# Output projection: four token tiles through both column halves, then the other four

## The chip, the core and the metric

The kernel runs on one core of a Trainium2 chip. The core has five engines that run side by side, each through its own list of instructions in order: TensorE (PE, matrix multiply; PEld is its weight load), VectorE (DVE), ScalarE (ACT), GpSimd (POOL), and SyncE (SP), which here issues every DMA. They wait for each other by semaphores. The metric is the device time of one execution in microseconds; three runs of the kernel before gave 1167.01 us in the median (1166.46 to 1168.68).

## The reference

One encoder block over 1024 tokens of width 1024, in float32:

```
n   = rms_norm(x, attn_norm_w)
y   = [ windowed attention with sink (8 heads) || bidirectional retention (8 heads) ] of n @ w_in
h   = x + y @ w_out                       # the output projection
m   = rms_norm(h, ffn_norm_w)
out = h + (silu(m @ w_gate) * (m @ w_up)) @ w_down
```

## The kernel before

**Split operands.** Every float32 operand of a large matmul is split into a high part (rounded) and a low part (what is left), and each product is three matmuls: high by high, high by low, low by high. So each block of weights (a granule, 128x512, 256 KB) is loaded by DMA into a tile `raw`, cast into `wh` (line 224), and `wl` = `raw` - `wh` is subtracted (line 229). Which engines do it is two letters: `W_MID` = "ap" is the cast on ACT and the subtraction on POOL; `W_HOLD` = "pd", used during attention, is POOL and DVE. There are 7 `raw` buffers and 10 pairs of `wh` and `wl`; a pair is free again when the last token tile that needs its granule has been through (line 272).

**The output projection.** The 1024 tokens are 8 tiles of 128. `w_out` has two halves of 512 columns, (O, 0) and (O, 1), with 8 granules each. A pass is one tile through one half: 8 granules of 3 matmuls, accumulated in one of three PSUM banks (names `o0_4`, `o1_4`: half 0 and 1 of tile 4). Before, all 8 tiles go through half 0, then all 8 through half 1, in the order `PAIRED` = 0, 4, 1, 5, 2, 3, 6, 7. `residual` (line 803) adds `x`, writes `h` to HBM and lets ACT sum the squares.

**The norm.** After a tile's second half `norm_rows` (line 837) forms the scale `hr` (DVE, DVE, POOL power), scales both halves of `h` on DVE, transposes them on PE (`pm`), and writes what the gate and up products read. Tiles 0 to 3 are copied to `stash` and split into `X_hi`, `X_lo`. Tile t of 4 to 7 is combined with tile t - 4 into the sums of Winograd's variant of Strassen's scheme: `t1` (in `stash`), `t2`, `t3`, `b22` and `t4`, split into `X` and the tiles T2, T3 and T4. `t4` and the low part of T4 are POOL's (lines 870 and 873), all other sums DVE's.

**Order.** A scheduler lays the instructions out at compile time by priority and a cost model; each engine then runs its list in order. The loop at line 1009 interleaves the projection with the norms: `fill` (line 285) lets PE do projection steps in between, `drain(prev)` puts in the transposes and sums of the tile before. `prepare` loads and splits the first gate and up weights (`A11`, `A12`, sums `S1` to `S4`). After it the products begin: `pa` and `pb` (A11, A12 against tiles 0 to 3), then `pa` with T2, `pc`, `pa` with T3, `pc`, `pa` with T4.

Of the kernel before, what the change touches and what calls it, by code (L numbers as in the profile page):

```python
# [12 lines left out]
ALU = mybir.AluOpType  # L13
# [6 lines left out]
NT = S // P  # L20
# [8 lines left out]
AX_BUFS = 5  # L29
W_FIRST = ("pp", "dd") * 4  # L30
W_MID = "ap"
W_HOLD = "pd"
ENG = {"a_rope": "d", "r_rope": "d", "a_vz": "d", "a_rv": "d", "a_kh": "a", "a_vh": "a", "a_kl": "d", "a_vl": "d",
       "a_kv": "a", "scan": "d", "r_vh": "a", "r_Rh": "da", "r_Rl": "pd", "r_vl": "p", "r_gw": "p", "r_qkh": "a",
# [2 lines left out]
       "o_c": "a", "o_h": "p", "o_l": "p", "y_h": "d", "m_h": "da"}  # L37
FILL = {"A": 2, "Aend": 7, "B1": 2, "B2": 5, "C1": 4, "C2": 4, "D0": 6, "D1": 2, "T1": 3, "O0": 4, "O1": 4, "O2": 3}
SOONER = {"w": -80, "exp": 10, "pass": 0}
PAIRED = (0, 4, 1, 5, 2, 3, 6, 7)  # L40
LEAD = 6
DOWN_LEAD = 5
RD_BUFS = 10
# [17 lines left out]
def hymba_block(ctx, tc, x, xT, cst, prm, retw, ffnw, wqkv, wkv, wout, wg, wu, wd, out):  # L61
# [35 lines left out]
    pe, act, dve, pool = (Engine(e) for e in (nc.tensor, nc.scalar, nc.vector, nc.gpsimd))  # L97
# [33 lines left out]
    def f32(ap):  # L131
        return ap.bitcast(F32)
# [4 lines left out]
    def mm_ps(name):  # L137
        return pp.tile([P, 512], F32, name=name, tag="mm", bufs=MM_BUFS)
# [15 lines left out]
    def four(v):  # L154
        return v[:].rearrange("p (j n) -> p j n", n=P)
# [32 lines left out]

    A, B, C, D, O = "a", "b", "c", "d", "o"
    src = {(A, 0): wqkv[0], (B, 0): wqkv[1], (A, 1): wqkv[2], (B, 1): wqkv[3], (C, 0): wkv, (D, 0): wqkv[4],  # L190
           (O, 0): wout[0], (O, 1): wout[1]}
    chunks = list(src)
    granules, first_granule = [], {}
    for c in chunks:
# [2 lines left out]
    seq = []  # L197
    for c in chunks:
        n = WIDE if seq else 3
        ts = PAIRED if c == (O, 1) else range(NT)  # L200
        seq += [(c, t, k) for k in range(8) for t in ts[:n]] + [(c, t, k) for t in ts[n:] for k in range(8)]
    W = []
    pos = [0]
# [1 line left out]
    hold = [False]  # L205
# [5 lines left out]
    def load_next():  # L211
        with sooner("w"):
            load_granule()

    def load_granule():
        i = len(W)
        raw = wp.tile([P, 512], F32, name=f"raw{i}", tag="raw", bufs=RAW_BUFS)
        hi = wp.tile([P, 512], F32R, name=f"wh{i}", tag="wh", bufs=W_BUFS)
        lo = wp.tile([P, 512], F32R, name=f"wl{i}", tag="wl", bufs=W_BUFS)
        nc.sync.dma_start(raw[:], granules[i])  # L220
        mode = W_FIRST[i] if i < 8 else W_HOLD if hold[0] else W_MID
        e1, e2 = mode
        if e1 == "a":
            act.copy(hi[:], raw[:])
        elif e1 == "d":
            dve.tensor_copy(hi[:], raw[:])
        else:
            pool.tensor_scalar(hi[:], raw[:], 1.0, 1.0, op0=ALU.mult, op1=ALU.mult)
        (dve if e2 == "d" else pool).tensor_tensor(lo[:], raw[:], f32(hi[:]), op=ALU.subtract)
        W.append((hi, lo))  # L230
# [12 lines left out]
    def sip():  # L243

        c, t, k = seq[pos[0]]
        per = 2 if c[0] == C else 1
        g = first_granule[c] + k // per
        i = part[0]
        if i == 0:
            while len(W) <= g:  # L250
                load_next()
            if c == chunks[0] and t == 0:
                split_x(k, 0)
            if k == 0:
                banks[c, t] = mm_ps(f"{c[0]}{c[1]}_{t}")
                begun[0] += 1
        width = 512 // per
        o = (k % per) * width
        lh, ll = (X[:, k, t * P:t * P + P] for X in (X_hi, X_lo))
        rh, rl = (w[:, o:o + width] for w in W[g])  # L260
        with sooner("pass"):
            pe.matmul(banks[c, t][:, :width], ll if i == 2 else lh, rl if i == 1 else rh,
                      start=k == 0 and i == 0, stop=k == 7 and i == 2)
        part[0] = (i + 1) % 3
        if i < 2:
            return
        pos[0] += 1
        if c == chunks[0] and t == 3:
            split_x(k, 1)
        if k == 7:  # L270
            done.add((c, t))
        if t == NT - 1 and (k + 1) % per == 0:
            freed[0] = g + 1
        if not hold[0] and pos[0] % PUMP == 0:
            pump(1)
# [9 lines left out]
    def fill(n):  # L285

        n = round(3 * n)
        while n and ready():
            sip()
            n -= 1  # L290

    def need(c, t):
        while (c, t) not in done:
            sip()
        return banks[c, t]
# [9 lines left out]
    def split_x(k, half):  # L305

        xv = xs[:, xcount[0] % 8, :]
        xcount[0] += 1
        nc.sync.dma_start(xv, xT[k][:, half * 512:half * 512 + 512])
        xh, xl = (X[:, k, half * 512:half * 512 + 512] for X in (X_hi, X_lo))  # L310
        act.activation(xh, xv, AF.Copy, scale=anw[:, k:k + 1])
        dve.scalar_tensor_tensor(xl, xv, anw[:, k:k + 1], f32(xh), op0=ALU.mult, op1=ALU.subtract)
# [209 lines left out]
    def drain(gen):  # L522
        for _ in gen:
            pass
# [7 lines left out]
    for g in range(2):  # L532
# [3 lines left out]
        prev = iter(())  # L536
        for t in range(NT):
            ps = need((A, g), t)
# [16 lines left out]
            prev = gen  # L555
# [5 lines left out]
        for c in range(NT):  # L561
            ps = need((B, g), c)
# [167 lines left out]
    prev = iter(())  # L730
    for t in range(NT):
        ps = need((C, 0), t)
# [9 lines left out]
        prev = gen  # L742
# [31 lines left out]
    for i in range(2 * NT):  # L774
        t, kv = divmod(i, 2)
# [26 lines left out]

    def residual(t, ch, xr, h):
        nc.sync.dma_start(xr[:], x[t * P:(t + 1) * P, ch * 512:ch * 512 + 512])
        ps = need((O, ch), t)
        dve.tensor_tensor(h[:], ps[:], xr[:], op=ALU.add)
        took()
        nc.sync.dma_start(Hd[t][ch][:], h[:])
        act.activation(xr[:], h[:], AF.Square, accum_out=hss[:, t, ch:ch + 1])

    for t in range(NT):
        residual(t, 0, U(f"xr{t}", TAG["xr"]), U(f"h{t}", "y"))
        fill(FILL["O0"])
    front.close()
# [13 lines left out]
    def T_(name, tag):  # L828
        return p2.tile([P, 512], F32, name=name, tag=tag, bufs=MID[tag])

    stash = {}

    def split_to(hi, lo, v, e_lo=None):
        act.activation(hi, v, AF.Copy)
        (e_lo or dve).tensor_tensor(lo, v, f32(hi), op=ALU.subtract)

    def norm_rows(t, h, hn):

        dve.tensor_tensor(hr[:, t:t + 1], hss[:, t, 0:1], hss[:, t, 1:2], op=ALU.add)
        dve.tensor_scalar(hr[:, t:t + 1], hr[:, t:t + 1], 1.0 / DM, EPS, op0=ALU.mult, op1=ALU.add)  # L840
        pool.tensor_tensor(hr[:, t:t + 1], hr[:, t:t + 1], mhalf[:, 0:1], op=ALU.pow)
        for a in range(2):
            dve.scalar_tensor_tensor(hn[a][:], h[a][:], hr[:, t:t + 1], ffnw_t[:, a * 512:a * 512 + 512],
                                     op0=ALU.mult, op1=ALU.mult)
        yield
        pts = []
        for a in range(2):
            pt = ax_ps(f"pm{t}_{a}")
            for j in range(4):
                pe.transpose(pt[:, j * P:j * P + P], hn[a][:, j * P:j * P + P], f32(ident[:]))  # L850
            pts.append(pt)
        if t < 4:
            for a in range(2):
                b = T_(f"stash{t}{a}", "four")
                act.activation(b[:], pts[a][:], AF.Copy)
                stash[t, a] = b
                split_to(*x_rows(t, 4 * a), four(pts[a]))
            return
        u = t - 4
        b11, b21 = stash[u, 0], stash[u, 1]  # L860
        t1, t4 = b11, b21
        b22, t2, t3 = (T_(f"{v}_{u}", "five") for v in ("b22", "t2", "t3"))
        to = lambda i: tuple(TT[i][:, v, :, u * P:u * P + P] for v in range(2))
        act.activation(b22[:], pts[1][:], AF.Copy)
        dve.tensor_tensor(t1[:], pts[0][:], b11[:], op=ALU.subtract)
        dve.tensor_tensor(t2[:], pts[1][:], t1[:], op=ALU.subtract)
        dve.tensor_tensor(t3[:], b22[:], pts[0][:], op=ALU.subtract)
        split_to(*to(2), four(t2))
        split_to(*x_rows(t, 0), four(t1))
        pool.tensor_tensor(t4[:], b21[:], t2[:], op=ALU.subtract)  # L870
        split_to(*to(3), four(t3))
        split_to(*x_rows(t, 4), four(b22))
        split_to(*to(4), four(t4), pool)


    def split(name, v):
# [129 lines left out]
        finish(unit, 1, 0, b1[:], None)  # L1006

    prev = iter(())
    for t in PAIRED:
        h = [T_(f"h{t}_{ch}", "four_") for ch in range(2)]  # L1010
        nc.sync.dma_start(h[0][:], Hd[t][0][:])
        xr = T_(f"xr{t}_1", "five")
        residual(t, 1, xr, h[1])
        gen = norm_rows(t, h, (h[0], xr))
        go(gen)
        if t == PAIRED[-2]:
            prepare(2)
        fill(FILL["O1"])
        drain(prev)
        fill(FILL["O2"])  # L1020
        prev = gen
# [82 lines left out]
    for i in range(4):  # L1104
        h = pd.tile([P, 512], F32, name=f"h21{i}", tag="hd", bufs=8)
# [70 lines left out]
```

## Time and profile before

| what | value |
|---|---|
| median of 3 runs | 1167.01 us |
| the profiled execution, its own time | 1167.41 us |
| span of its profile | 1165.6 us |
| PE busy | 1128.6 us (97%) |
| DVE busy | 833.0 us (71%) |
| ACT busy | 548.2 us (47%) |
| POOL busy | 248.2 us (21%) |
| mean granted clock of TensorE | 0.991 |

The projection's matmuls run from 401.9 to 524.0 us, the first of them between those of attention, which ends at about 452 us. From 555 us on PE is busy in 606.8 of 610.6 us. An operation's duration in the trace includes its fill, so matmuls that follow each other closely are read by the distance of their starts.

### The profile page before, as it was taken

To read this page: it belongs to the slowest core of one execution; us is meant where nothing else is said; L and a number is where in the kernel's file an instruction comes from. 1 tells how busy PE (TensorE), PEld (TensorE's weight loads), DVE (VectorE), ACT (ScalarE), POOL (GpSimd) and SP (SyncE) were. 2 spreads that over 40 slices of the span, in tenths; PEclk is the share of its full clock that TensorE was granted. 3 is DMA by queue.
4 is the path that set the end of the run, shared out by engine and by line. 5 is a ranking of instruction groups with operands and counts; after the bars stand their busy time and mean duration, and the time that the engine had idled before them with its cause. 6 is when DMAs were issued, how large, how long until landed. Compare 5 with 4: busy or idle time off the path is not lost.

```text
span 1165.6 us, 16106 instructions
## 1 busy us (share of the span) xinstructions
PE 1128.6 (97%) x5384; PEld 928.2 (80%) x5384; DVE 833.0 (71%) x1632; ACT 548.2 (47%) x1134; POOL 248.2 (21%) x308
## 2 busy tenths in 40 slices
PE   8989998998999999998999999999999999999998
PEld 6767787787978887876888888888888888888887
DVE  6988876888889994589766676677657755555553
ACT  4744544445478874346334333433333334454441
POOL 3345734358545631322000000000000000000000
PEclk9989999999999999999999999999999999999999
DMA  8520112003100023631534554456445768776672
GB/s 288 200 73 1 37 37 62 12 1 91 37 1 2 19 73 109 192 115 55 188 120 153 190 173 134 136 181 188 144 120 173 231 217 278 232 231 190 216 266 71
DMA packets 82594, 152.59 MB, mean 131 GB/s; under 512 B 9424, under 2 KB 9936, under 8 KB 82512
## 3 DMA queue, kind: packets, MB, share of 16 engines
q1 hardware_dynamic: 82512, 151.57, 40.6%
q8 instruction: 42, 0.69, 0.2%
q14 instruction: 40, 0.33, 0.1%
HBM read 111.43 MB, written 40.11 MB: 130 GB/s over the span
## 4 chain that ended last, share of the span: by engine, by line
PE 70%; DVE 16%; issue 5%; POOL 5%; DMA 3%; ACT 1%; SPq 0%; POOLq 0%; DVEq 0%; ACTq 0%
PE pa L88 20%; PE da L88 10%; PE pc L88 10%; PE dc L88 5%; PE pb L88 5%; PE a L88 4%; PE o L88 4%; PE db L88 3%; PE d L88 3%; PE c L88 1%; DVE X_lo L88 1%; PE b L88 1%; POOL Y L88 1%; DMA xs<-in_xT_dram 1%; DVE h L88 1%
## 5 line engine op out<-in xcount | busy, mean ns | idle before, releaser
L91 POOL TENSOR_TENSOR wl<-raw,wh 128x512 fp32r<-128x512 f32 x44 | 60.0, 1389 | 60.8 <-ACT wh L91 60.4
L88 PE MATMUL b<-wh,X_hi 128*128 128x512 f32 x128 | 53.8, 420 | 0.0
L88 PE MATMUL b<-wh,X_lo 128*128 128x512 f32 x128 | 52.7, 412 | 0.0
L88 PE MATMUL a<-wh,X_lo 128*128 128x512 f32 x128 | 51.1, 400 | 1.7 <-DVE X_lo L88 1.6
L88 PE MATMUL a<-wh,X_hi 128*128 128x512 f32 x128 | 50.7, 396 | 1.9 <-DVE krv L88 1.9
L88 PE MATMUL b<-wl,X_hi 128*128 128x512 f32 x128 | 52.1, 407 | 0.0
L88 PE MATMUL o<-wh,X_hi 128*128 128x512 f32 x128 | 51.1, 399 | 0.0
L88 PE MATMUL a<-wl,X_hi 128*128 128x512 f32 x128 | 50.9, 397 | 0.0
L88 PE MATMUL o<-wh,X_lo 128*128 128x512 f32 x128 | 50.2, 392 | 0.0
L88 PE MATMUL o<-wl,X_hi 128*128 128x512 f32 x128 | 50.1, 392 | 0.0
L88 DVE TENSOR_TENSOR S<-A,A 128x512 f32<-128x512 f32 x44 | 31.3, 711 | 3.1 <-DMA A<-in_wg_dram 2.2
L91 ACT CAST wh<-raw 128x512 fp32r<-128x512 f32 x44 | 26.2, 616 | 10.1 <-PE o L88 4.6
L88 PEld LDWEIGHTS a<-wh,X_lo 128*128 128x128 f32 x128 | 24.3, 190 | 7.9 <-DVE X_lo L88 3.4
L88 PEld LDWEIGHTS a<-wh,X_hi 128*128 128x128 f32 x128 | 24.2, 189 | 6.9 <-issue 2.5
L88 PEld LDWEIGHTS b<-wh,X_lo 128*128 128x128 f32 x128 | 25.1, 196 | 5.3
L88 ACT ACTIVATE sg<-sg 128x512 f32<-128x512 f32 x33 | 20.8, 631 | 17.7 <-DVE sg L88 17.7
L88 PEld LDWEIGHTS b<-wl,X_hi 128*128 128x128 f32 x128 | 25.5, 199 | 4.4
L88 PEld LDWEIGHTS b<-wh,X_hi 128*128 128x128 f32 x128 | 25.7, 201 | 4.0
L88 PEld LDWEIGHTS a<-wl,X_hi 128*128 128x128 f32 x128 | 24.4, 190 | 4.7 <-DVE wl L88 0.4
L88 PEld LDWEIGHTS o<-wh,X_lo 128*128 128x128 f32 x128 | 24.0, 188 | 4.6
L88 PEld LDWEIGHTS o<-wh,X_hi 128*128 128x128 f32 x128 | 24.1, 188 | 4.4
L88 PEld LDWEIGHTS o<-wl,X_hi 128*128 128x128 f32 x128 | 24.1, 188 | 4.2
(2950 smaller groups left out, 3786.3 us busy)
## 6 DMA issues: line engine op xcount, KB each, us to landing
A<-in_wg_dram SPq DMA_DIRECT2D x44, 256.0 KB, 2.9
A<-in_wu_dram SPq DMA_DIRECT2D x44, 256.0 KB, 3.1
R<-in_wd_dram SPq DMA_DIRECT2D x44, 256.0 KB, 2.7
L_S<-LS SPq DMA_DIRECT2D x44, 256.0 KB, 2.3
R_T<-RT SPq DMA_DIRECT2D x44, 256.0 KB, 2.1
raw<-in_wqkv_dram SPq DMA_DIRECT2D x40, 256.0 KB, 2.9
L_A<-a SPq DMA_DIRECT2D x33, 256.0 KB, 2.3
xs<-in_xT_dram SPq DMA_DIRECT2D x16, 256.0 KB, 5.2
```

The costliest lines, as they stand in the source:

```text
L88: ins = fn(*args, **kw)
L91: ins = fn(*args, **kw)
```

## The change

Tiles 0, 4, 1, 5 (`EARLY`) go through both halves first, then 2, 3, 6, 7 (`LATE`). The list of chunks becomes (O, 0) and (O, 1) for `EARLY`, (O, 2) and (O, 3) for `LATE`, where (O, 2) is half 0 and (O, 3) half 1 again: 32 granules in place of 16, so 16 more DMAs, casts and subtractions. All splits of these granules outside attention are now "ad": the cast on ACT, the subtraction on DVE. And `t4` and the low part of T4 move from POOL to DVE. The passes and the order of the norms (0, 4, 1, 5, 2, 3, 6, 7) stay.

```diff
+W_OUT = "ad"
-PAIRED = (0, 4, 1, 5, 2, 3, 6, 7)
+EARLY, LATE = (0, 4, 1, 5), (2, 3, 6, 7)
...
-           (O, 0): wout[0], (O, 1): wout[1]}
+           (O, 0): wout[0], (O, 1): wout[1], (O, 2): wout[0], (O, 3): wout[1]}
+
+    tiles = {c: (EARLY, EARLY, LATE, LATE)[c[1]] if c[0] == O else tuple(range(NT)) for c in src}
...
-        mode = W_FIRST[i] if i < 8 else W_HOLD if hold[0] else W_MID
+        mode = W_FIRST[i] if i < 8 else W_HOLD if hold[0] else W_OUT if i >= first_granule[O, 0] else W_MID
...
-        if t == NT - 1 and (k + 1) % per == 0:
+        if t == tiles[c][-1] and (k + 1) % per == 0:
...
-        ps = need((O, ch), t)
+        ps = need((O, ch + 2 * (t in LATE)), t)
...
-    for t in range(NT):
+    for t in EARLY:
         residual(t, 0, U(f"xr{t}", TAG["xr"]), U(f"h{t}", "y"))
...
-        pool.tensor_tensor(t4[:], b21[:], t2[:], op=ALU.subtract)
+        dve.tensor_tensor(t4[:], b21[:], t2[:], op=ALU.subtract)
...
-        split_to(*to(4), four(t4), pool)
+        split_to(*to(4), four(t4))
...
-    for t in PAIRED:
+    for t in EARLY + LATE:
+        if t == LATE[0]:
+            for u in LATE:
+                residual(u, 0, T_(f"xr{u}_0", "five"), T_(f"h{u}_0", "four_"))
+                fill(FILL["O1"])
+                drain(prev)
+                fill(FILL["O2"])
```

In the lists of instructions below, `o1_5` is half 1 of tile 5, `o2_2` half 0 of tile 2 (chunk (O, 2)) and `o3_2` its half 1; `wh64`, `wl64` are granule 64; helper lines 88 and 91 are 89 and 92 in the changed kernel.

DVE, the norms of tiles 4 and 5, before:

```order
L88 TENSOR_TENSOR stash00_5658<-pm4_0_5704,stash00_5658 128x512
L88 TENSOR_TENSOR t2_0_5715<-pm4_1_5709,stash00_5658 128x512
L88 TENSOR_TENSOR t3_0_5716<-b22_0_5714,pm4_0_5704 128x512
L88 TENSOR_TENSOR X_lo_94<-stash00_5658,X_hi_93 128x4x128
L88 TENSOR_TENSOR T2_5436<-t2_0_5715,T2_5436 128x4x128
L88 TENSOR_TENSOR T3_5437<-t3_0_5716,T3_5437 128x4x128
L88 TENSOR_TENSOR X_lo_94<-b22_0_5714,X_hi_93 128x4x128
L88 TENSOR_TENSOR h5_1_5742<-o1_5_5691,xr5_1_5744 128x512
```

The same place of DVE's list in the changed kernel:

```order
L89 TENSOR_TENSOR stash00_5546<-pm4_0_5604,stash00_5546 128x512
L92 TENSOR_TENSOR wl63_5600<-raw63_5598,wh63_5599 128x512
L89 TENSOR_TENSOR t2_0_5615<-pm4_1_5609,stash00_5546 128x512
L89 TENSOR_TENSOR t3_0_5616<-b22_0_5614,pm4_0_5604 128x512
L89 TENSOR_TENSOR X_lo_94<-stash00_5546,X_hi_93 128x4x128
L89 TENSOR_TENSOR T2_5312<-t2_0_5615,T2_5312 128x4x128
L89 TENSOR_TENSOR stash01_5550<-stash01_5550,t2_0_5615 128x512
L89 TENSOR_TENSOR T3_5313<-t3_0_5616,T3_5313 128x4x128
L89 TENSOR_TENSOR X_lo_94<-b22_0_5614,X_hi_93 128x4x128
L89 TENSOR_TENSOR T4_5314<-stash01_5550,T4_5314 128x4x128
L89 TENSOR_TENSOR h5_1_5648<-o1_5_5579,xr5_1_5650 128x512
```

The two sums of POOL (`stash01`, T4) and a weight split now stand in DVE's list, ahead of the next tile's residual.

DVE, from the residual of tile 2 to that of tile 3, both of half 1, before:

```order
L88 SCALAR_TENSOR_TENSOR xr2_1_5800<-h2_1_5798,hr_5201,ffnw_t_2983 128x512
L88 TENSOR_TENSOR stash10_5780<-pm5_0_5826,stash10_5780 128x512
L88 TENSOR_TENSOR t2_1_5837<-pm5_1_5831,stash10_5780 128x512
L88 TENSOR_TENSOR t3_1_5838<-b22_1_5836,pm5_0_5826 128x512
L88 TENSOR_TENSOR X_lo_94<-stash10_5780,X_hi_93 128x4x128
L88 TENSOR_TENSOR T2_5436<-t2_1_5837,T2_5436 128x4x128
L88 TENSOR_TENSOR T3_5437<-t3_1_5838,T3_5437 128x4x128
L88 TENSOR_TENSOR X_lo_94<-b22_1_5836,X_hi_93 128x4x128
L88 TENSOR_TENSOR h3_1_5864<-o1_3_5813,xr3_1_5866 128x512
```

The same two residuals in the changed kernel:

```order
L89 TENSOR_TENSOR S4_00_6181<-A12_00_6033,S2_00_6151 128x512
L89 TENSOR_TENSOR h2_1_5916<-o3_2_5881,xr2_1_5918 128x512
L89 TENSOR_TENSOR hr_5201<-hss_5200 128x1
L89 TENSOR_SCALAR hr_5201<-hr_5201 128x1
L89 SCALAR_TENSOR_TENSOR h2_0_5915<-h2_0_5915,hr_5201,ffnw_t_2983 128x512
L89 SCALAR_TENSOR_TENSOR xr2_1_5918<-h2_1_5916,hr_5201,ffnw_t_2983 128x512
L89 TENSOR_TENSOR h3_1_5960<-o3_3_5937,xr3_1_5962 128x512
```

The seven sums of tile 5 between them have moved ahead, past the four passes of chunk (O, 2).

PE, the start of chunk (O, 2) in the changed kernel, where the granules of half 0 are needed for the second time:

```order
L89 MATMUL o2_2_5663<-wh63_5599,X_lo_94 128x512
L89 MATMUL pm1_0_5682<-ident_75,h1_0_5563 128x128 x4
L89 MATMUL pm1_1_5687<-ident_75,xr1_1_5566 128x128 x4
L89 MATMUL o2_2_5663<-wh64_5642,X_hi_93 128x512
L89 MATMUL o2_3_5736<-wh60_5481,X_hi_93 128x512
L89 MATMUL o2_3_5736<-wl60_5482,X_hi_93 128x512
L89 MATMUL o2_3_5736<-wh60_5481,X_lo_94 128x512
L89 MATMUL o2_3_5736<-wh61_5496,X_hi_93 128x512
L89 MATMUL o2_3_5736<-wl61_5497,X_hi_93 128x512
L89 MATMUL o2_2_5663<-wl64_5643,X_hi_93 128x512
```

Here the pass of tile 3 starts before that of tile 2 is through; before, passes were not interleaved in this part of PE's list. The first four pairs of `pm` stand about 100 rows earlier in PE's list than before, the last four where they stood.

## Rows read from the trace of the kernel before

**Rows 1.** The page: busy time by engine, and what went to and from HBM.
```profile
PE 1128.6 (97%) x5384; PEld 928.2 (80%) x5384; DVE 833.0 (71%) x1632; ACT 548.2 (47%) x1134; POOL 248.2 (21%) x308
...
HBM read 111.43 MB, written 40.11 MB: 130 GB/s over the span
```

**Rows 2.** Windows: start:end, length, busy us (instructions) by engine, PE clock, DMA share, GB/s.
```profile
504.00:520.00 16.00, 14.48 (x72) 11.79 (x70) 12.56 (x20) 7.64 (x17) 4.27 (x5) 1.00 0.36 118
520.00:531.00 11.00, 8.84 (x37) 6.62 (x38) 10.11 (x20) 8.63 (x19) 0.55 (x1) 0.84 0.23 73
531.00:555.00 24.00, 21.70 (x98) 17.06 (x97) 21.70 (x33) 13.79 (x24) 6.34 (x5) 1.00 0.17 55
```

**Rows 3.** Chain of waits, 440 to 520 us: start, length, what, xcount.
```profile
450.12 28.39 PE o L88 x125
```

**Rows 4.** Timeline of PE, 505 to 562 us: start, length, operation, [idle before <-releaser].
```profile
511.99 0.60 PE L88 MATMUL pm<-ident,h 128*128 128x128 f32 x4
...
512.78 0.48 PE L88 MATMUL o<-wh,X_hi 128*128 128x512 f32 x1
...
518.10 0.39 PE L88 MATMUL o<-wh,X_lo 128*128 128x512 f32 x1
520.30 0.63 PE L88 MATMUL pm<-ident,h 128*128 128x128 f32 x4 [1.82 <-ACT X_hi L88]
...
523.97 0.39 PE L88 MATMUL o<-wh,X_lo 128*128 128x512 f32 x1
525.22 0.66 PE L88 MATMUL pm<-ident,h 128*128 128x128 f32 x4 [0.87 <-DVE h L88]
...
527.69 0.80 PE L88 MATMUL pa<-X_lo,A_00h 128*128 128x512 f32 x1 [0.86 <-DVE X_lo L88]
...
530.42 0.63 PE L88 MATMUL pa<-X_lo,A_00h 128*128 128x512 f32 x1
...
535.87 0.63 PE L88 MATMUL pm<-ident,xr 128*128 128x128 f32 x4 [0.70 <-DVE xr L88]
...
543.70 0.50 PE L88 MATMUL pa<-T,S_00h 128*128 128x512 f32 x1 [1.35 <-DVE T L88]
...
554.89 0.73 PE L88 MATMUL pa<-T,A_00h 128*128 128x512 f32 x2 [0.24 <-DVE sg L88]
```

**Rows 5.** Timeline of DVE at the same columns, attention's end and 505 to 562 us.
```profile
448.02 1.29 DVE L91 TENSOR_TENSOR q71pl<-q71p,q71ph 128x512 fp32r<-128x512 f32 x2 [2.20 <-ACT q71ph L91]
...
512.69 1.41 DVE L88 TENSOR_TENSOR X_lo<-stash,X_hi 128x512 fp32r<-128x512 f32 x1
514.02 2.37 DVE L88 TENSOR_TENSOR T<-t,T 128x512 fp32r<-128x512 f32 x2
...
516.92 0.68 DVE L88 TENSOR_TENSOR h<-o,xr 128x512 f32<-128x512 f32 x1
...
519.40 0.75 DVE L88 SCALAR_TENSOR_TENSOR h<-h,hr,ffnw_t 128x512 f32<-128x512 f32 x1 [0.66 <-POOL hr L88]
...
526.95 1.28 DVE L88 TENSOR_TENSOR X_lo<-pm,X_hi 128x512 fp32r<-128x512 f32 x2
...
528.75 0.68 DVE L88 TENSOR_TENSOR h<-o,xr 128x512 f32<-128x512 f32 x1
...
542.97 0.68 DVE L88 TENSOR_TENSOR T<-t,T 128x512 fp32r<-128x512 f32 x1
```

**Rows 6.** Timeline of POOL, 505 to 562 us.
```profile
512.26 1.29 POOL L88 TENSOR_TENSOR stash<-stash,t 128x512 f32<-128x512 f32 x1 [2.92 <-DVE t L88]
514.29 1.56 POOL L88 TENSOR_TENSOR T<-stash,T 128x512 fp32r<-128x512 f32 x1 [0.74 <-ACT T L88]
```

**Rows 7.** Groups by form, 440 to 560 us: operation xcount | busy, mean ns | idle before.
```profile
L91 POOL TENSOR_TENSOR wl<-raw,wh 128x512 fp32r<-128x512 f32 x6 | 8.4, 1447 | 15.1 <-ACT wh L91 15.1
...
L91 ACT CAST wh<-raw 128x512 fp32r<-128x512 f32 x6 | 3.4, 617 | 4.7 <-PE o L88 4.6
```

**Rows 8.** DMA issues: operation xcount, KB each, median us to landing.
```profile
raw<-in_wout_dram SPq DMA_DIRECT2D x16, 256.0 KB, 2.8
```

More of the change, by code (lines that the diff above doesn't have):

```diff
@@ L199, in hymba_block @@
         n = WIDE if seq else 3
-        ts = PAIRED if c == (O, 1) else range(NT)
+        ts = tiles[c]
         seq += [(c, t, k) for k in range(8) for t in ts[:n]] + [(c, t, k) for t in ts[n:] for k in range(8)]
@@ L831, in hymba_block, with split_to @@
     stash = {}
-    def split_to(hi, lo, v, e_lo=None):
+    def split_to(hi, lo, v):
         act.activation(hi, v, AF.Copy)
-        (e_lo or dve).tensor_tensor(lo, v, f32(hi), op=ALU.subtract)
+        dve.tensor_tensor(lo, v, f32(hi), op=ALU.subtract)
     def norm_rows(t, h, hn):
@@ L1015, in hymba_block @@
         go(gen)
-        if t == PAIRED[-2]:
+        if t == LATE[2]:
             prepare(2)
```

## The prediction

> **What bounds the kernel now.** I read the busy times first: PE is busy for 97% of the span [rows 1], so a change pays only where PE waits or runs slowly. The windows show where that is: three stretches between 504 and 555 us, in which PE is busy for 45.0 us of 51, one of them at a granted clock of 0.84, so partly at 1.2 of 2.4 GHz; DVE is busy for 44.4 us there, in the middle for 10.1 of 11 [rows 2]. The chain of waits gives the pace without waits: 125 matmuls of the projection in 28.39 us [rows 3], 0.227 each, so 5.45 us for a pass of 24.
>
> PE's timeline says what it waits for [rows 4]. From the transposes at 511.99 to the product with T4 at 554.89 us are 42.90 us. The work in it is 132 matmuls (24 + 12 + 24 + 24 + 48) by 0.227, which is 30.0, and four pairs of transposes by 0.79 (511.99 to 512.78), which is 3.2: together 33.1. So 9.8 us are lost. The waits listed are 1.82, 0.87, 0.86, 0.70, 1.35 and 0.24, 5.8 in all; 1.4 is the slow clock (six matmuls from 527.69 to 530.42 take 2.73 in place of 1.36, after PE had waited three times in 10 us); the rest is slow transposes and restarts at the waits.
>
> These waits end with DVE, or with ACT behind DVE. The pass of tile 3 through half 1 ends at 509.3 us (12 matmuls before the transposes at 511.99), but DVE adds its residual only at 516.92 [rows 5], since the sums of tile 5 stand ahead of it in DVE's list. The last pass ends at 524.2; its residual comes at 528.75, 4.5 us late. DVE carries a backlog from tile 5 into the last four norms.
>
> **The change, part by part.** *The norms of tiles 0, 4, 1, 5 move ahead of four passes.* PE's list keeps its passes and transposes; the first four pairs of transposes stand earlier, the last four where they were. In DVE's list the seven sums of tile 5 no longer stand between the residuals of tiles 2 and 3: chunk (O, 2), four passes, lies between. I price a sum or split on DVE at 0.60 (two X_lo and one more fill 526.95 to 528.75 [rows 5]) and count from T, the start of `o1_5`. DVE has `wl67` done at T + 17.1 (below), then ten operations to the residual of tile 3 (T + 23.1), then it waits for PE; `wl70` to `wl75` follow the release of their buffers until T + 31.0, and seven operations, residual and gate weights, end at T + 35.2. PE ends `o3_2` at T + 36.2: 6.2 for `o1_5` with a pair of transposes, five passes, two pairs, 1.1 of waits. So DVE meets the last four norms without a backlog.
>
> *The last four norms* I walk from E, the end of `o3_7`. The residual of tile 6 comes as its pass ends, at E - 6.2; squares, `hr` and scalings take 3.9, two splits and two X_lo 2.4: X_lo of tile 3 is there at E, PE wants it at E + 1.0, so the waits at 525 and 527 go, and that at 520 for the same reason a pass earlier. The scaled tile 7 follows at E + 5.3 (one split in hand, five sums, two scalings by 0.67, two tiny ones, 0.2 for POOL); PE wants it at 0.79 + 5.45 = E + 6.2: the wait at 535 goes. T2 of tile 7 is 14 sums later, E + 13.7; PE wants it at 6.2 + 0.79 + 5.45 + 0.23 = E + 12.6. So a wait of 1.1 stays at T2, between 0 (if 0.54 is the pace) and 2.5 (if each takes the 0.68 that one lasts alone). The wait for `sg` goes, since DVE's list now has it ahead of the next unit's first sum. Gain in this stretch: 9.8 - 1.1 = 8.7, at full clock, as the one wait left is shorter than that of 1.35 at 543.70, after which the clock held [rows 2, 4].
>
> *t4 and the low part of T4 go from POOL to DVE*, two operations by 0.60 for each of four tiles. POOL's two, of 1.29 and 1.56 [rows 6], cost DVE more: beside them one X_lo takes 1.41 in place of 0.68, and two T take 2.37 in place of 1.28 [rows 5], 1.8 together. So 1.2 replaces 1.8. This is already in the walk, which has no POOL work but `hr`.
>
> The Trainium skill ("SBUF — State Buffer", section "Who interferes with whom") says that a VectorE operation with two SBUF inputs and a GpSimd operation that reads SBUF shut each other out for a whole instruction. By that rule DVE would lose up to 1.29 + 1.56 = 2.85 for a tile and the move would gain 1.65, not 0.6; the rows bear out two thirds of it.
>
> *16 more granules.* At the end of attention 54 and 55 are split while DVE stands idle for 2.20 us [rows 5]; their two casts (617 ns each [rows 7]) stand ahead of the ACT copy for which DVE waits there: 0.4 us of delay, between 0 and 0.8. From half 1 to (O, 2) it is tight. Granules 62 to 67 come free one by one during `o1_5`, with the sums of tile 4 between them on DVE. Up to `wl64` DVE has 14 operations by 0.60, two scalings, two tiny ones, and about 1.6 us of waits for the freed buffer, the squares and POOL's power (0.66 [rows 5]): T + 11.7. PE wants `wl64` after 42 matmuls and two pairs of transposes, T + 11.1: a wait of 0.7 with the semaphore. Then the scaled half of tile 5 is 0.3 late and `wl66` 0.15. Together 1.15, between 0 and 3 (14 operations at 0.68 add 1.1, a second late granule the rest). At the step to (O, 3) `wl75` is done at T + 31.0 and PE reaches it at T + 34. POOL's subtractions of 1447 ns [rows 7] go; nothing waits for it then. Granules 44 and 45 put two splits more on DVE before attention and take two from POOL: 0, between -0.5 and 1.2.
>
> *The loads.* 16 DMAs of 256 KB, landing in 2.8 us [rows 8], stand in SP's list between the loads of `x` and `h`. Seven raw buffers run ahead and hide them; the tightest is granule 69, whose issue stands behind a load of `h` that waits for the transposes of tile 4: landing at T + 7, cast at T + 8.7. Without that cover each late load costs PE up to 2.8.
>
> **The sum.** -8.7 + 1.15 + 0.4 = -7.15 us. The profiled execution took 1167.41 (1165.6 of span and 1.8 around it), so 1160.3; the median is 0.4 below that execution, so 1160.0 rounded. After 555 us PE's work follows without gaps, so nothing there gives it back.
>
> **The rivals.**
>
> A. *No new wait at the granules and none at T2:* -9.8, so 1157.2. For it: the walk misses by tenths. Against: DVE's list is dense there.
>
> B. *DVE stays late at the end.* Only the first two waits go (from 518.3 to 520.30 and 524.2 to 525.22, 3.0 together [rows 4]), the three more sums in the last chain add 1.8 at T2 and the granules cost 1.55: +0.35, so 1167. For it: the residual that is 4.5 us late now. Against: tile 5, which makes it late, is out of the way.
>
> C. *The granules make DVE the bound in the middle: slower.* The place is `h1_1` to `wl67`, with 20 sums and splits between PE and its weights. Were they as slow as those beside POOL, three in 3.78, so 1.26 each [rows 5], they would take 13.2 us more, and PE would wait for all of it: 1173. It decides for slower from 9.3 us of waits on, 0.46 more on each. Against: POOL has no sum then.
>
> D. *The traffic bounds.* 16 by 262144 bytes are 4.2 MB, at the mean of 130 GB/s [rows 1] 32 us, so 1199. Against: the DMA share is 0.17 to 0.36 in the three stretches [rows 2]. The Trainium skill ("SBUF — State Buffer", section "A bandwidth-pool intuition that's wrong") says that HBM is almost always the bottleneck from end to end; PE's 97% speaks against it here.
>
> **How the numbers follow.** Forecast 0.64, with its own range of 1158 to 1163.5 (the terms at their ends, or 1.4 us of slow clock at the new waits), A 0.12, B 0.14, C 0.08, D 0.02. The range of 1157.4 to 1166.3 takes in nearly all of A and the lower part of B. No change means within 0.2%, 2.3 us, about what a measurement of this kernel can tell. Faster: the forecast, A and a little of B, 0.80; same: the rest of B, 0.11; slower: C and D but for a mild C, 0.09.
>
> **What would show it.** PE without a wait of over 0.3 us before the transposes of tiles 2, 3, 6 and 7; one of about 1 us at T2 and one of about 0.7 at `wl64`; DVE at 0.60 a sum with nothing on POOL but `hr`; a granted clock near 1.0 from 440 to 560 us. I would be wrong if PE waits for `wl` at most granules, if the residual of tile 7 is late again, or if the clock falls in the middle.

## The result and the profile after

| | us, median | lowest to highest | runs |
|---|---|---|---|
| before | 1167.51 | 1166.46 to 1168.68 | 4 |
| after | 1160.58 | 1160.23 to 1161.78 | 4 |

The ratio is 0.9942, with a 95% interval of 0.9925 to 0.9959. The profiled execution of after took 1161.78 us, 1.2 above the median, of which 1160.0 are its span. Part of that arose where the two kernels still do the same: at 305 us PE stands 1.04 us behind the execution of before (the transposes `k5pt` begin at 306.15 against 305.11). So the two traces differ by less than the medians do (5.6 against 6.9 us), and I compare stretches.

The page (as in [rows 1]) shows 32 more operations on DVE (the splits of 16 more granules, those of 8 granules that POOL had before, and POOL's 8 operations for t4 and T4), 16 fewer on POOL, and 4.2 MB more read:
```profile
PE 1127.6 (97%) x5384; PEld 929.2 (80%) x5384; DVE 841.7 (73%) x1664; ACT 557.0 (48%) x1150; POOL 226.8 (20%) x292
...
HBM read 115.62 MB, written 40.11 MB: 134 GB/s over the span
```
The windows of after (columns as in [rows 2]; the last is cut at the product with T4, 5.5 us earlier than before):
```profile
480.00:504.00 24.00, 22.98 (x105) 18.63 (x104) 21.50 (x38) 13.43 (x28) 0.55 (x1) 1.00 0.76 247
504.00:520.00 16.00, 16.00 (x77) 13.32 (x76) 8.82 (x17) 4.46 (x10) 1.10 (x2) 1.00 0.52 173
520.00:531.00 11.00, 11.00 (x59) 9.23 (x58) 10.23 (x21) 9.37 (x20) 1.10 (x2) 1.00 0.13 47
531.00:549.40 18.40, 17.70 (x81) 14.19 (x80) 18.12 (x31) 12.15 (x20) 0.00 (x0) 1.00 0.22 72
```
PE is busy without a gap from 504 to 531 us, where it lost 3.7 us in [rows 2], and the granted clock is 1.00 throughout. What it lost anew is in the first row: 1.0 of 24 us. The timeline of PE in after, against [rows 4], says where:
```profile
450.57 0.39 PE L92 MATMUL q71o<-q71pl,V 128*128 128x512 f32 x1
...
455.79 0.50 PE L89 MATMUL o<-wl,X_hi 128*128 128x512 f32 x1 [0.49 <-DVE wl L92]
...
482.04 0.50 PE L89 MATMUL o<-wl,X_hi 128*128 128x512 f32 x1 [1.02 <-DVE wl L92]
...
514.56 0.60 PE L89 MATMUL pm<-ident,h 128*128 128x128 f32 x4
...
520.90 0.60 PE L89 MATMUL pm<-ident,h 128*128 128x128 f32 x4
...
524.54 0.60 PE L89 MATMUL pm<-ident,h 128*128 128x128 f32 x4
...
525.65 0.40 PE L89 MATMUL pa<-X_lo,A_00h 128*128 128x512 f32 x1
...
531.32 0.60 PE L89 MATMUL pm<-ident,xr 128*128 128x128 f32 x4
...
538.82 0.50 PE L89 MATMUL pa<-T,S_00h 128*128 128x512 f32 x1 [0.63 <-DVE T L89]
...
549.42 0.62 PE L89 MATMUL pa<-T,A_00h 128*128 128x512 f32 x2
```
The four pairs of transposes and the first X_lo have no bracket any more: nothing is waited for. Three waits are left, at `wl57` (44 matmuls ahead of the first transposes, at 465.90), at `wl64` and at T2 of tile 7. I cut this part of the program in two with such rows. The *middle* runs from the last `q71o` of attention (450.57 here) to the transposes of tile 2 (514.56), the *tail* from there to the product with T4 (549.42). In before the middle begins with this row:
```profile
449.73 0.39 PE L91 MATMUL q71o<-q71pl,V 128*128 128x512 f32 x1
```
Middle and tail took 62.26 (449.73 to 511.99) and 42.90 us there [rows 4], in after 63.99 and 34.86: -8.04 + 1.73 = -6.3 us.

DVE in after, against [rows 5]:
```profile
453.35 4.79 DVE L92 TENSOR_TENSOR wl<-raw,wh 128x512 fp32r<-128x512 f32 x6
462.02 0.69 DVE L89 TENSOR_TENSOR h<-o,xr 128x512 f32<-128x512 f32 x1 [3.87 <-DMA xr<-in_x_dram]
...
481.31 0.68 DVE L92 TENSOR_TENSOR wl<-raw,wh 128x512 fp32r<-128x512 f32 x1
...
518.37 0.69 DVE L89 TENSOR_TENSOR h<-o,xr 128x512 f32<-128x512 f32 x1 [0.38 <-PE o L89]
...
538.09 0.68 DVE L89 TENSOR_TENSOR T<-t,T 128x512 fp32r<-128x512 f32 x1
```
The residual of tile 6 (518.37) now waits for PE: DVE is on time. The second row was not expected: the residual of tile 0 waits 3.87 us for a load.

### The profile page after: what moved, and what is told of

The parts are those of the page before. It is cut to its first block, busy times and chain, and to the rows that moved or that the text cites. A ratio compares the mean times of both kernels' runs of the same rounds, so it can differ in the third digit from the quotient of the medians.

```text
span 1160.0 us, 16183 instructions
## 1 busy us (share of the span) xinstructions
PE 1127.6 (97%) x5384; PEld 929.2 (80%) x5384; DVE 841.7 (73%) x1664; ACT 557.0 (48%) x1150; POOL 226.8 (20%) x292
## 4 chain that ended last, share of the span: by engine, by line
PE 72%; DVE 15%; issue 4%; POOL 4%; ACT 1%; DMA 1%; SPq 0%; POOLq 0%; ACTq 0%; DVEq 0%
PE pa L89 20%; PE pc L89 10%; PE da L89 10%; PE o L89 5%; PE dc L89 5%; PE pb L89 5%; PE a L89 4%; PE db L89 3%; PE d L89 3%; PE c L89 1%; PE b L89 1%; POOL Y L89 1%; DMA xs<-in_xT_dram 1%; DVE X_lo L89 1%; DVE krv L89 1%
## 5 line engine op out<-in xcount | busy, mean ns | idle before, releaser
L92 POOL TENSOR_TENSOR wl<-raw,wh 128x512 fp32r<-128x512 f32 x36 | 49.1, 1388 | 45.8 <-ACT wh L92 45.5
L92 ACT CAST wh<-raw 128x512 fp32r<-128x512 f32 x60 | 35.1, 616 | 9.1 <-PE o L89 3.6
```

The source lines that it names most:

```text
L92: ins = fn(*args, **kw)
```

## The experiments

The change holds three edits: the order of the passes, t4 with the low part of T4 from POOL to DVE ("t4"), and the granules' low parts from POOL to DVE ("granules"). Ratios are to the kernel before, measured beside each run (its median was 1166.68 to 1167.51 us), with their 95% intervals. Middle and tail are read as above, from the one execution of each kernel that was profiled. The times hold more than these two stretches: in the traces of the old order the last `q71o` comes anywhere from 447.62 (best_old) to 450.90 us (t4_alone).

| run | order | t4 | granules | us | ratio | middle | tail |
|---|---|---|---|---|---|---|---|
| before | old | POOL | POOL | 1167.08 | 1 | 62.26 | 42.90 |
| t4_alone | old | DVE | POOL | 1163.54 | 0.9965 (0.9952 to 0.9977) | 62.17 | 37.85 |
| old_dd | old | DVE | DVE | 1161.76 | 0.9954 (0.9942 to 0.9967) | 62.17 | 36.50 |
| order_alone | new | POOL | POOL | 1170.28 | 1.0026 (1.0015 to 1.0036) | 70.49 | 36.86 |
| t4_back | new | POOL | DVE | 1165.41 | 0.9987 (0.9978 to 0.9995) | 65.22 | 36.83 |
| wl_back | new | DVE | POOL | 1170.77 | 1.0031 (1.0020 to 1.0043) | 73.44 | 34.90 |
| after | new | DVE | DVE | 1160.58 | 0.9942 (0.9925 to 0.9959) | 63.99 | 34.86 |

**order_alone: only the order.**
```diff
-W_OUT = "ad"
+W_OUT = "ap"
...
-        dve.tensor_tensor(t4[:], b21[:], t2[:], op=ALU.subtract)
+        pool.tensor_tensor(t4[:], b21[:], t2[:], op=ALU.subtract)
...
-        split_to(*to(4), four(t4))
+        split_to(*to(4), four(t4), pool)
```


> The new order of the passes with both other edits undone: the low parts of the projection's granules and t4 with the low part of T4 go to POOL again. Theory of the prediction (the order takes tile 5's sums out of DVE's way): the four late residuals are on time and most of the 8 us of the last four norms are still gained, but POOL needs 1.45 us a granule where PE asks for one every 0.68 us at the start of half 1; granules 54 to 59 and the two operations of y of tile 7 make about 11 us on POOL, so wl59 is 3 to 5 us late, and the POOL work beside the sums costs 1 to 2 us more. 1165 us (1162 to 1167). Rival 1 (what pays is that t4 leaves POOL, the order nothing): 1167 or more, with the waits before the transposes of tiles 3 and 6 still there. Rival 2 (the edits beside the order cost and gain nothing): 1160.6.

1170.28 us, 5 above the expected 1165: the order by itself makes the kernel slower. The tail gains 6.0 us, most of what the order was meant to give, and the waits before the transposes of tiles 3 and 6, by which rival 1 was to be known, are gone. The middle loses 8.2, and not at `wl59`: PE waits 1.85 us for the scaled `h` of tile 0 (467.01) and 1.78 and 0.70 for POOL's `wl` (486.47, 488.15), and the clock falls behind these waits, as the windows show (columns as in [rows 2]):
```profile
463.00:475.00 12.00, 10.11 (x42) 7.93 (x41) 7.00 (x14) 5.03 (x12) 2.06 (x3) 0.86 0.47 141
485.00:500.00 15.00, 12.82 (x52) 10.24 (x53) 11.92 (x16) 7.29 (x16) 8.94 (x7) 0.89 0.48 159
```

**t4_alone: only t4.**
```diff
-        pool.tensor_tensor(t4[:], b21[:], t2[:], op=ALU.subtract)
+        dve.tensor_tensor(t4[:], b21[:], t2[:], op=ALU.subtract)
...
-        split_to(*to(4), four(t4), pool)
+        split_to(*to(4), four(t4))
```


> The kernel before with one edit only: t4 and the low part of T4 on DVE. Theory of the prediction: each of the four tiles frees 0.6 us of DVE (1.2 in place of 1.8 lost beside POOL); tile 5's residual chain is 0.6 to 1.2 us earlier, the waits of 1.82 and 1.35 us shrink by that: 1166 us (1165 to 1167.3), the waits before the transposes and at X_lo stay. Rival 1 (the move off POOL is what pays): 1160 to 1162. By the rule of a port that shuts out a whole instruction, 1.65 a tile: 1164.

1163.54 us: two operations a tile, moved, bring half of the whole gain in the old order, and in the trace 5.05 us of the tail. (The medians show 3.5; the last `q71o` came 1.17 us later in this execution than in before.) The theory's 1166 is 2.5 too high, rival 1's 1160 to 1162 too low; the port's 1164 comes nearest, though the trace shows other causes beside a port. The PE timeline of this run, to be held against [rows 4]; the wait of 1.82 before the second transposes is gone though the order is the old one:
```profile
513.07 0.60 PE L88 MATMUL pm<-ident,h 128*128 128x128 f32 x4
...
519.40 0.60 PE L88 MATMUL pm<-ident,h 128*128 128x128 f32 x4
...
524.88 0.66 PE L88 MATMUL pm<-ident,h 128*128 128x128 f32 x4 [1.56 <-DVE h L88]
```
Why 5 us, where two by 0.6 had been priced? In the trace of before, POOL's queue at tile 6 and what DVE does then:
```profile
531.44 1.30 POOL L88 TENSOR_TENSOR stash<-stash,t 128x512 f32<-128x512 f32 x1 [7.06 <-DVE hr L88]
532.69 0.55 POOL L88 TENSOR_TENSOR hr<-hr,mhalf 128x1 f32<-128x1 f32 x1
533.48 1.69 POOL L88 TENSOR_TENSOR T<-stash,T 128x512 fp32r<-128x512 f32 x1 [0.23 <-ACT T L88]
```
```profile
533.28 0.75 DVE L88 SCALAR_TENSOR_TENSOR h<-h,hr,ffnw_t 128x512 f32<-128x512 f32 x1 [1.33 <-POOL hr L88]
533.95 1.77 DVE L88 SCALAR_TENSOR_TENSOR xr<-h,hr,ffnw_t 128x512 f32<-128x512 f32 x1
```
The power for `hr` of tile 7 stands behind t4 in POOL's list, so DVE idles for 1.33 us, and then its scaling takes 1.77 in place of 0.75 beside the low part of T4. These 2.4 us lie on the path to the scaled tile 7 (PE's wait of 0.70 at 535.87 and the 1.35 behind it in [rows 4]). Tiles 4 and 5 make the residuals later by the priced difference: from the residual of tile 1 to that of tile 2 DVE takes 15.03 us in before (491.86 to 506.89) and 14.42 in t4_alone (492.84 to 507.26). From there to that of tile 3 it takes 10.03 and 8.62, since the low part of T4 now stands behind that residual in its list. And the clock stays at 1.00 from 520 to 531 us in t4_alone, where it was 0.84 [rows 2], so the 1.4 us of slow matmuls are gone as well.

**t4_back: after, with t4 on POOL.** The diff of the first experiment without `W_OUT`.

> The changed kernel with one edit undone: t4 and the low part of T4 on POOL again. Theory: DVE loses 0.6 us more for each of tiles 4 to 7; at T2 of tile 7 only that of tile 6 lies ahead, so the wait there grows from 0.63 to about 1.2 us; at wl64 that of tile 4 lies ahead or beside, +0.6 there: 1161.8 us (1160.8 to 1163). X_lo or T beside POOL's operations 1.2 to 1.4 us in place of 0.68. Rival 1 (the move off POOL is what pays): 1166 to 1167.

1165.41 us, 4.8 above after, where 1.2 was expected. The same queue shows in the new order, and at `wl64`, behind the sums of tile 4, PE waits 2.42 in place of 1.02:
```profile
530.74 0.75 DVE L89 SCALAR_TENSOR_TENSOR h<-h,hr,ffnw_t 128x512 f32<-128x512 f32 x1 [1.32 <-POOL hr L89]
531.40 1.76 DVE L89 SCALAR_TENSOR_TENSOR xr<-h,hr,ffnw_t 128x512 f32<-128x512 f32 x1
```
```profile
481.60 0.50 PE L89 MATMUL o<-wl,X_hi 128*128 128x512 f32 x1 [2.42 <-DVE wl L92]
...
533.31 0.63 PE L89 MATMUL pm<-ident,xr 128*128 128x128 f32 x4 [1.05 <-DVE xr L89]
```
Middle and tail account for 3.2 of the 4.8 (1.23 and 1.97); the execution profiled took 1164.37, and the others scatter from 1162.67 to 1166.89. Where the other 1.6 arise is not shown.

**wl_back: after, with the granules' low parts on POOL** (`W_OUT = "ap"`).

> The changed kernel with one edit undone: the low parts of the projection's granules on POOL again. Theory: six granules by 1.45 us and y of tile 7 on POOL make wl59 3 to 5 us late at the start of half 1 (PE's first waits there 0.5 us now); from half 1 to (O, 2) POOL has wl64 to wl67 ready earlier than DVE has them now, so the wait of 1.0 us at wl64 goes, but the sums beside POOL are slower and the scaled tile 5 is up to 1.5 us late: 1164 us (1161.5 to 1166). Rival 2 (it does not matter which engine splits, PE never waits for it): 1160.6 within 0.7. Rival 3 (DVE is what is short in the middle, POOL relieves it): 1159.3, without the wait at wl64.

1170.77 us, 10 above after, and not where it was expected: PE waits 0.73 for one `wl`, but 2.44 and 3.71 for the scaled `h`. DVE, POOL and PE in this run:
```profile
463.29 0.69 DVE L89 TENSOR_TENSOR h<-o,xr 128x512 f32<-128x512 f32 x1 [10.98 <-DMA xr<-in_x_dram]
...
482.42 1.78 DVE L89 TENSOR_TENSOR stash<-stash,t 128x512 f32<-128x512 f32 x1
484.13 1.76 DVE L89 TENSOR_TENSOR T<-t,T 128x512 fp32r<-128x512 f32 x1
485.81 1.78 DVE L89 TENSOR_TENSOR X_lo<-b,X_hi 128x512 fp32r<-128x512 f32 x1
487.52 1.77 DVE L89 TENSOR_TENSOR T<-stash,T 128x512 fp32r<-128x512 f32 x1
```
```profile
481.96 6.79 POOL L92 TENSOR_TENSOR wl<-raw,wh 128x512 fp32r<-128x512 f32 x4 [1.50 <-ACT wh L92]
```
```profile
466.69 0.63 PE L89 MATMUL pm<-ident,h 128*128 128x128 f32 x4 [2.44 <-DVE h L89]
...
492.58 1.08 PE L89 MATMUL pm<-ident,h 128*128 128x128 f32 x4 [3.71 <-DVE h L89]
```
Two mechanisms. First, the load of x for tile 0 stands in SP's list behind loads of granules, which wait for raw buffers that POOL's splits hold; the residual waits for it. Second, four sums on DVE and four splits on POOL take turns: 1.70 us a pair, where DVE alone needs 0.60 and POOL 1.26. The clock adds to both: it stands at 0.86 and 0.77 in the windows of the two waits, partly at 1.2 of 2.4 GHz.
```profile
463.00:475.00 12.00, 9.53 (x40) 7.52 (x39) 7.37 (x14) 5.43 (x13) 2.41 (x3) 0.86 0.47 140
485.00:500.00 15.00, 10.90 (x40) 8.85 (x41) 13.44 (x20) 6.97 (x15) 4.29 (x4) 0.77 0.50 156
```

**old_dd: the old order with both edits.** t4_alone, and in `load_granule`:
```diff
-        mode = W_FIRST[i] if i < 8 else W_HOLD if hold[0] else W_MID
+        mode = W_FIRST[i] if i < 8 else W_HOLD if hold[0] else "ad" if i >= first_granule[O, 0] else W_MID
```


> The kernel before in its own order of passes, with the two edits beside the order: t4 and the low part of T4 on DVE, the low parts of the projection's 16 granules on DVE. With the run that had only the first of these (1163.5 us) and the changed kernel (1160.6) it prices the order by itself. Theory: granules cost nothing in the old order, where DVE is idle beside them: 1163.5 us (1162.6 to 1164.3), so that the order is worth 2.9 us once both edits are there. Rival (the order is worth nothing, the granules' move does it): 1160.6.

1161.76 us, between what the theory (1163.5) and the rival (1160.6) had. Its interval overlaps that of after, and the traces give nearly the same sum: 62.17 + 36.50 = 98.67 against 63.99 + 34.86 = 98.85. With both edits made, the order takes 1.6 off the tail and puts 1.8 on the middle; that it is worth anything by itself is not shown (the medians are 1.2 us apart).

**late5: is it tile 5?**
```diff
-EARLY, LATE = (0, 4, 1, 5), (2, 3, 6, 7)
+EARLY, LATE = (0, 4, 1), (5, 2, 3, 6, 7)
-        if t == LATE[2]:
+        if t == LATE[-2]:
```


> The changed kernel with tile 5 moved from the early four to the late ones: early 0, 4, 1, late 5, 2, 3, 6, 7; the weights are still loaded and split twice, and DVE still does t4 and the granules. Theory (the sums of tile 5 between the late residuals make the backlog): from the transposes of tile 2 to the product with T4 it takes 37.9 us, as in the old order with t4 on DVE, in place of 34.9, a wait of about 1.6 before the transposes of tile 6 is back; at wl64 nothing changes: 1163.6 us (1162 to 1165). Rival (the distance that the second loading of the weights puts between the parts, not tile 5, is what helps): 1160.6 within 0.8.

1164.88 us (ratio 0.9980, 0.9971 to 0.9989), the expected time for another reason. The tail is 35.71, 0.85 above after and not 3. The rest was lost before the middle begins: with three early passes, the last `q71o` comes at 454.30, 3.7 later than in after. Of these 3.7, 0.5 were there at `q70p`; 3.2 arise behind it, where PE waits for POOL's `q71sm`. Its two operations take 3.58 in place of 0.94, the first of them 3.13, while four splits go through DVE at 0.62 each:
```profile
446.18 3.58 POOL L89 TENSOR_SCALAR q71sm<-q71sm,q71den 128x256 f32<-128x256 f32 x2 [3.36 <-ACT xr L89]
```
```profile
446.48 2.48 DVE L92 TENSOR_TENSOR wl<-raw,wh 128x512 fp32r<-128x512 f32 x4
```
```profile
449.37 1.19 PE L92 MATMUL q71p<-ident,q71sm 128*128 128x128 f32 x7 [1.98 <-POOL q71sm L89]
```
So the time does not tell the theories apart; the tail speaks against a backlog that is tile 5's alone.

**x_early: the kernel before with one load moved ahead.**
```diff
+XP = 400
...
-        nc.sync.dma_start(xr[:], x[t * P:(t + 1) * P, ch * 512:ch * 512 + 512])
+        with tc.high_priority(XP if ch and t == PAIRED[0] else 0):
+            nc.sync.dma_start(xr[:], x[t * P:(t + 1) * P, ch * 512:ch * 512 + 512])
...
-        xr = T_(f"xr{t}_1", "five")
+        xr = wp.tile([P, 512], F32, name=f"xr{t}_1", tag="raw", bufs=RAW_BUFS) if t == PAIRED[0] else T_(f"xr{t}_1", "five")
```


> The kernel before with one load moved: that of x for the residual of tile 0 in half 1 is issued some 25 us earlier, into a buffer of the granules' loads; in the kernel before it stands in SP's list behind loads that wait for buffers, lands at 482.9 us and makes that residual 4.6 us late (pass ended at 478.3). Theory A (the backlog of DVE starts with this load and is carried to the end): the residual comes at 478.5, that of tile 1 1.5 us earlier (then it waits for PE), so the residual of tile 3 1.5 us earlier and the wait of 1.82 before the transposes of tile 3 is 0.3 to 0.5: 1165.4 us (1164.6 to 1166.3). Theory B (the backlog comes from the sums of tiles 4 and 5 alone, as the prediction has it): 1166.9, all waits as before.

1165.52 us, ratio 0.9987 (0.9979 to 0.9996), tail 41.16. Theory A had it, to the wait:
```profile
519.37 0.63 PE L89 MATMUL pm<-ident,h 128*128 128x128 f32 x4 [0.43 <-ACT X_hi L89]
```
In before, DVE's residuals of tiles 0, 1 and 2 stand so:
```profile
482.95 0.69 DVE L88 TENSOR_TENSOR h<-o,xr 128x512 f32<-128x512 f32 x1 [2.98 <-DMA xr<-in_x_dram]
...
491.86 0.68 DVE L88 TENSOR_TENSOR h<-o,xr 128x512 f32<-128x512 f32 x1
...
506.89 0.68 DVE L88 TENSOR_TENSOR h<-o,xr 128x512 f32<-128x512 f32 x1
```
The first waits for the load. From the second to the third, two tiles, DVE takes 15.0 us, where two passes of PE with their transposes take 12.7 (a pass: 513.07 to 519.40 in t4_alone), so what is late at tile 1 stays late to the end. Without the late load 1.7 of the tail's 9.8 lost us go. The 1.35 between t4_alone and old_dd have the same source, as far as the traces tell: with the splits on DVE, raw buffers come free sooner, and the residual of tile 0 comes at 480.64 in place of 483.93, while PE is only 0.57 ahead.

**after_x: the same move in after** (`EARLY[0]` for `PAIRED[0]`).

> The changed kernel with the same load moved ahead. In the changed kernel that residual comes at 462.0 us, 4.3 after its pass (457.7), since the load stands in SP's list behind loads of granules that wait for buffers; the residual of tile 1 is 1.5 late by it. Theory A (the wait of 1.0 us at wl64 is this lateness, carried through DVE's list): wl64 is 1.2 to 1.5 us earlier, the wait there goes or is under 0.3: 1159.4 us (1158.8 to 1160.2). Theory B (wl64 waits for the sums of tile 4 in DVE's list, whatever the load does): 1160.6, the wait of 1.0 stays.

The wait at `wl64` falls from 1.02 to 0.35, nearly as theory A had it (under 0.3):
```profile
479.64 0.50 PE L90 MATMUL o<-wl,X_hi 128*128 128x512 f32 x1 [0.35 <-DVE wl L93]
```
Middle and tail shrink by 0.7 together. The time, 1160.12 us (0.9944, 0.9931 to 0.9958), can't tell that from after.

**defer and defer_y: the two other waits.**
```diff
-        dve.tensor_tensor(t4[:], b21[:], t2[:], op=ALU.subtract)
...
-        split_to(*to(4), four(t4))
...
+        def fourth():
+            dve.tensor_tensor(t4[:], b21[:], t2[:], op=ALU.subtract)
+            split_to(*to(4), four(t4))
+        later.append(fourth)
```
The list `later` is run where the expectation says. defer_y has beside it the low part of tile 7's y on DVE.

> The changed kernel, with t4 and the low part of T4 of each tile issued later: those of tiles 4 and 5 after the residual of tile 2's half 0, those of tiles 6 and 7 after the sums of tile 7. Nothing is added or taken away. In DVE's list wl64 stands two operations earlier and T2 of tile 7 one or two earlier. Theory (the two waits that are left are DVE's list, operation by operation at 0.60 us): the wait of 1.02 at wl64 goes (1.2 us earlier, wanted 1.2 earlier), that of 0.63 at T2 shrinks to 0 to 0.3: 1159.0 us (1158.3 to 1159.8), from the stretch before (O, 3) -1.2 and from the last four norms -0.5. Rival (the release of the buffer or the cast on ACT sets wl64, not DVE's list): 1160.3 to 1160.8, the wait at wl64 stays.

> As the run before, and the low part of tile 7's y goes to DVE in place of POOL. In the changed kernel it takes 1.68 us on POOL while DVE splits granules 56 to 61, six in 4.79 us in place of 3.68, and PE waits 0.49 for one of them. Theory (POOL's operation holds up DVE's beside it by 1.1 us, 0.60 replaces that): the wait of 0.49 goes, another 0.5 less: 1158.5 us (1157.8 to 1159.3). Rival (these granules are late because they are split after y and the residual, whoever splits y): no difference to the run before, or 0.6 more.

In defer the wait at T2 is gone and that at `wl64` is halved (tail 33.86, middle 63.59), but the five runs scatter from 1158.64 to 1161.48 and the ratio, 0.9947 (0.9933 to 0.9961), shows no gain where 1159.0 was expected. With y's low part on DVE the six splits take 3.69 us in place of 4.79 and the first wait goes too: 1158.50 us, 0.9930 (0.9917 to 0.9942), as expected.

**best_old and best_new: the remedies together, in either order.** best_old is old_dd with t4 and the low part of T4 issued later, as in defer, and the load of x ahead, as in x_early. best_new is defer_y with the edit of after_x; y's low part on DVE is in best_new alone.

> A version in the old order of passes, weights loaded once: both edits on DVE as in the run old_dd (1161.8 us), t4 and the low part of T4 issued later, the load of x early. Theory: the waits of 0.6 and 0.6 at T2 of tile 7 shrink to 0.2 or less, that of 0.3 before the transposes of tile 6 goes: 1160.0 us (1159 to 1161). If the order by itself is worth something beyond the edits, it stays 1.5 us or more above the run best_new.

> A version in the new order with all that the runs pointed to: t4 and the low part of T4 later, the low part of tile 7's y on DVE, the load of x early. The run without the last (defer_y) took 1158.5 us with one wait of 0.4 at a granule. Theory A (that wait is the late load's): 1158.0 us (1157.3 to 1158.7). Theory B: 1158.5, the wait stays.

1159.13 us (0.9932, 0.9920 to 0.9945; middle 62.12, tail 35.65) and 1158.12 us (0.9925, 0.9912 to 0.9937; 62.46 and 33.84). The waits of PE from 440 to 565 us in best_new are these:
```profile
PE o L90 <- DVE wl L93: 0.3, 1, 0.3
PE q70o L93 <- DVE q70pl L93: 0.2, 1, 0.2
```
It has the lowest median of all runs, 2.5 us below after, with intervals that overlap. The time is theory A's, but the wait at `wl64` has only fallen from 0.41 in defer_y to 0.28. That the new order beats the old one is not shown here either: 1.0 us lies within both intervals, and the two differ in y's low part too, whose move took 1.0 us off the middle from defer to defer_y.

## Why the prediction was right, and where it was not

*The time* came out as forecast: 1160.0 against 1160.58. The sum nearly did: -8.04 in the tail for -8.7, and 0.1 at the end of attention (`q70p` to the last `q71o`, 10.50 before and 10.61 after) with +1.73 in the middle, for +1.55. That is -6.2 us for -7.15. The medians differ by 6.9, nearer to the forecast than the stretches do; that last bit is scatter, and so luck.

*The walk of DVE's list* held to within a microsecond. From T = 469.5, `wl64` was done at T + 12.5 for T + 11.7, `wl75` at T + 31.8 for T + 31.0. From E = 524.5, the residual of tile 6 came at E - 6.1 for E - 6.2, T2 at E + 14.3 for E + 13.7. All of "what would show it" is there: no wait before the four transposes, 0.63 at T2 (1.1 forecast), 1.02 at `wl64` (0.7), DVE at 0.60 a sum, a clock of 1.00. Rivals A to D don't show; D's traffic is there (a DMA share of 0.76 from 480 to 504 us), and none of PE's waits there ends with a load. The 0.7 us that the tail missed are not the wait at T2, which was in the sum. With that wait gone the tail still takes 33.84 (best_new): the work of 33.1, summed from matmuls and transposes, is 0.7 too low, as PE also loses a little where it restarts.

*The step that failed* is the attribution: "DVE carries a backlog from tile 5 into the last four norms", which the order was to cure, with t4's move a side gain of 0.6 a tile. The backlog is real, and the order by itself does take 6.04 us off the tail (order_alone). But t4's move by itself takes 5.05 (t4_alone), and the load of x moved ahead 1.74 (x_early). Together that is 12.8, more than the 9.8 that were lost, so the cures overlap, and the loss can't be divided among them. Beside t4's move and the granules' move, which take 6.40 with a middle as before (old_dd), the order takes only 1.64 more and gives it back in the middle. The direct price of t4's move was right (0.61 from 15.03 to 14.42). What that price left out are the power for `hr` behind t4 in POOL's list, the slow clock that goes with the waits, and a DVE list that is slower than PE's (15.0 us for 12.7) and so never wins back what it lost. The late load of x is in no part of the prediction.

*The loads*: "Seven raw buffers run ahead and hide them" failed in part: what they delay is the load of x behind them in SP's list, and through it 0.7 us at `wl64`. *The cast ahead of `q71ph`* cost 0.1 and not 0.4; a wait of 0.49 that the sum didn't have came at granule 57, whose split runs beside POOL's X_lo of y, and went when that moved to DVE (defer_y). *The granules on POOL* were booked as work that may "go; nothing waits for it then". Left on POOL in the new order they cost 10 us (wl_back), so that edit is the one on which the order depends.

## What to carry to other kernels

Before crediting a reordering, ask what the small edits beside it do alone: here the order by itself was slower, and the edits alone gave the gain within the error. Two cures of one loss can't be added up. A helper engine's operation can cost more than its neighbour's slowdown: read what stands behind it in its own list. Where an engine's list is no faster than the one it feeds, look for the first late item, which may be a load tens of microseconds earlier.

## What the runs showed of the hardware

In wl_back DVE and POOL took turns one for one when both had full lists of operations with two inputs in SBUF: 1.70 us a pair, near the 0.60 and 1.26 that the two take alone. Turns are not the rule everywhere: in late5 four splits went through DVE at 0.62 each while one operation of POOL took 3.13. Operations of DVE with an input in PSUM were not slowed: in wl_back two `q71pl` (input `q71p` in PSUM) took 1.28 us in the midst of six splits on POOL, which took 1.26 each:
```profile
448.26 1.28 DVE L92 TENSOR_TENSOR q71pl<-q71p,q71ph 128x512 fp32r<-128x512 f32 x2
```
```profile
446.31 7.57 POOL L92 TENSOR_TENSOR wl<-raw,wh 128x512 fp32r<-128x512 f32 x6 [0.87 <-ACT wh L92]
```
The Trainium skill ("SBUF — State Buffer", section "Who interferes with whom") says that a VectorE instruction with at most one SBUF input, outside the two-port modes, doesn't contend with GpSimd and that the lock is exclusive. Both agree with the rows of wl_back, better than the single pairs from which the prediction read two thirds.

In wl_back the wait of 2.44 us, the only one of PE since 449 us, was followed by six matmuls at 0.44 us each (468.08 to 470.72; 0.227 otherwise); in [rows 4] three waits of under 2 us stood ahead of the slow matmuls. The wait of 2.42 us in t4_back (481.60) was followed by none: the next matmuls start 0.23 us apart, and the granted clock is 1.00. Behind one of 1.85 us in order_alone (467.01) they start 0.43 apart until 471.27. So the length of the single wait doesn't decide it in these runs, and what does stays open.
